# Gates of the expert lookup: hi and lo weights side by side in one product, one-hots from single-input operations, GELU kept in PSUM

## The chip, the cores and the metric

One core of one Trainium2 chip runs the whole program. The metric is the device time of one execution in microseconds (us), and smaller is better. The engines that matter here are TensorE (PE in the rows; its weight loads are PEld), VectorE (DVE), ScalarE (ACT) and GpSimd (POOL). SP issues most of the DMAs. SBUF is the working memory, PSUM the small memory into which TensorE writes its products, in eight banks of 512 float32 per partition.

## The reference

The program is two blocks of a network on 256 tokens of width 1024. Only the last part of the second block, a lookup of experts called PEER, is touched by the change. Cut to what matters:

```python
v1, i1 = lax.top_k(s1, 16)                 # 8 heads, 128 keys in each of two lists
v2, i2 = lax.top_k(s2, 16)
cand_s = v1[..., :, None] + v2[..., None, :]
cand_i = i1[..., :, None] * 128 + i2[..., None, :]
top_s, pos = lax.top_k(cand_s, 16)         # 16 experts per head, 128 per token
experts = take_along_axis(cand_i, pos)
gates = softmax(top_s)
u = u_tab[experts]                         # 16384 experts of width 1024
act = gelu(einsum('ced,cd->ce', u, x)) * gates
out = einsum('ce,ced->cd', act, v_tab[experts])
```

So each token has 128 gates, each for one of 128 x 128 experts (first index i1, second index i2).

## The kernel before, in words

The kernel does not gather. It computes the GELU of all 16384 experts for all 256 tokens (stage "U"), multiplies by a dense array of gates that is zero for experts that were not selected, and multiplies the result with the whole second table (stage "V"). The dense array is `big`, 128 partitions (i2) by 128 (i1) by 256 tokens, float32 in SBUF.

Stage U is the loop of `peer` over pairs of i1 (64 iterations). Each iteration loads two blocks of the table (L1507), splits each into a rounded part and a rest (ScalarE L1509; the rest on VectorE for three eighths and on GpSimd for five eighths, both L1511) and lets TensorE make 48 matmuls of 256 columns into one PSUM bank (L1514, recorded at L163). Then come GELU and the product with the gates: for the `n` tokens whose gates are there already, ScalarE writes GELU into an SBUF tile `tmp` (L1518) and VectorE multiplies it into `big` (L1519). For the other tokens ScalarE writes GELU straight into `big` (L1521), and the gates are multiplied in later.

Selection and gates are a generator (`select`, which hands over to `gates` once per half of 128 tokens) that runs beside stage U: after each iteration `spend(2.81)` lets it do a few steps, and a group of four tokens in `gates` counts as 1.8, so about 1.56 groups are done per iteration. The order in time is: selection of the first half (before and at the start of stage U), 32 gate groups, selection of the second half, 32 gate groups. All of it is in order on each engine's queue; the tile framework may move an instruction within the queue when it plans the program, not while it runs.

For a token the gate array is a product: a matrix with a one at (slot, i2) against a matrix with the gate's weight at (slot, i1), summed over the 128 slots on the partitions. `hots` (L1465) makes these matrices for four tokens at once with four operations of VectorE on 128 x 512 float16, each with two SBUF inputs: the comparison with i1 (L1469), that times the upper part of the weight (L1470) and times its rest (L1471), and the comparison with i2 (L1472). The four tokens are interleaved, so a token's matrix has a step of four elements. `fill` (L1475) is done one group later: two accumulating matmuls of 128 columns per token, upper part and rest, into one PSUM bank (L1478, L1479, recorded at L163 as `y<-s`), then VectorE multiplies the first `n` rows of i1 (those whose GELU is there) into `big` (L1483) and ScalarE copies the other rows into `big` (L1485). Both write `big` with a step of 256 elements.

PSUM is two pools of four banks: `ps` for stage U's products, `acc` (tile name `y`) for the rest.

Of the kernel before, what the change touches and what calls it, by code (L numbers as in the profile page):

```python
# [8 lines left out]
F32 = mybir.dt.float32  # L9
# [4 lines left out]
F16 = mybir.dt.float16  # L14
AF = mybir.ActivationFunctionType
OP = mybir.AluOpType
# [3 lines left out]
P = 128  # L20
S = 256
# [26 lines left out]
PK = 128  # L48
# [6 lines left out]
class Net:  # L55
# [1338 lines left out]
    def select(self, s12, eT):  # L1394


        nc, V = self.nc, self.nc.vector
        tk = self.tk
        for t in range(T):
# [44 lines left out]
            pe = self.acc.tile([P, 512], F32, name="y").rearrange("p (j s) -> p j s", j=4)  # L1444
            for j in range(3):
                self.transpose(pe[:, j], et[:, j].rearrange("p h s -> p (h s)"))
            e = eT[:, :, t * P:t * P + P]
            V.tensor_copy(e[:, 0:2], pe[:, 0:2])
            f = tk.tile([P, P], F32, name="cand")
            V.tensor_scalar(f, pe[:, 2], 2.0 ** 15, None, op0=OP.mult)  # L1450
            V.tensor_copy(e[:, 2], f)
            V.tensor_tensor(e[:, 3], f, e[:, 2], op=OP.subtract)
            yield 2.0
            yield from self.gates(t, eT)

    def gates(self, t, eT):


        nc, V = self.nc, self.nc.vector
        if t == 0:  # L1460
            buf = self.tk.tile([P, 2048], F32, name="s", bufs=2)
            self.tmp.append(buf[:, :512])
            self.hot = buf[:, 512:].bitcast(F16).rearrange("p (r j n q) -> p r j n q", r=2, n=PK, q=4)

        def hots(t4):  # L1465

            o2, oh, ol = (self.hot[:, t4 // 4 % 2, j] for j in range(3))
            of = lambda j: eT[:, j, None, t4:t4 + 4].to_broadcast([P, PK, 4])
            V.tensor_tensor(ol, self.iota4, of(0), op=OP.is_equal)  # L1469
            V.tensor_tensor(oh, ol, of(2), op=OP.mult)  # L1470
            V.tensor_tensor(ol, ol, of(3), op=OP.mult)  # L1471
            V.tensor_tensor(o2, self.iota4, of(1), op=OP.is_equal)  # L1472
            return o2, oh, ol

        def fill(t4, o2, oh, ol):  # L1475
            pg = self.acc.tile([P, 512], F32, name="y").rearrange("p (q n) -> p q n", q=4)
            for q in range(4):
                self.mm(pg[:, q], o2[:, :, q], oh[:, :, q], True, False)  # L1478
                self.mm(pg[:, q], o2[:, :, q], ol[:, :, q], False, True)  # L1479
            n = self.ready  # L1480
            sl = self.big[:, :, t4:t4 + 4].rearrange("p i t -> p t i")
            if n:
                V.tensor_tensor(sl[:, :, :n], pg[:, :, :n], sl[:, :, :n], op=OP.mult)  # L1483
            if n < PK:
                nc.scalar.copy(sl[:, :, n:], pg[:, :, n:])  # L1485
            self.gated = t4 + 4
        late = None
        for t4 in range(t * P, t * P + P, 4):
            h = hots(t4)
            if late:  # L1490
                fill(*late)
            late = (t4,) + h
            yield 1.8
        fill(*late)

    def peer(self, hn, big, out):

        nc, V = self.nc, self.nc.vector
        U, W = self.io["peer_u"], self.io["peer_v"]
        self.big, self.ready, self.gated = big, 0, 0  # L1500
        self.tmp = [self.tk.tile([P, 512], F32, name="tmp")]
        self.phase("U")
        for i in range(0, PK, 2):
            ps = self.psum((P, 2, S))
            for q in range(2):
                ur = self.up.tile([P, KB, P], F32, name="raw")
                nc.sync.dma_start(ur, U[i + q])  # L1507
                up = self.pp.tile([P, 2, KB, P], F32R, name="pair")
                nc.scalar.copy(up[:, 0], ur)  # L1509
                for eng, ks in ((V, slice(0, UD)), (nc.gpsimd, slice(UD, KB))):  # L1510
                    lo = eng.tensor_tensor(up[:, 1, ks], ur[:, ks], up[:, 0, ks].bitcast(F32), op=OP.subtract)  # L1511
                    at = lo if eng is V else at
                for k in range(KB):
                    self.mm3(ps[:, q], (up[:, 0, k], up[:, 1, k]), (hn[0][:, k], hn[1][:, k]), k == 0, k == 7)  # L1514
            n = self.gated
            if n:
                tmp = self.tmp[i // 2 % 2].rearrange("p (q s) -> p q s", q=2)[:, :, :n]
                nc.scalar.activation(tmp, ps[:, :, :n], AF.Gelu_apprx_tanh)  # L1518
                V.tensor_tensor(big[:, i:i + 2, :n], tmp, big[:, i:i + 2, :n], op=OP.mult)  # L1519
            if n < S:  # L1520
                nc.scalar.activation(big[:, i:i + 2, n:], ps[:, :, n:], AF.Gelu_apprx_tanh)  # L1521
            self.ready = i + 2
            with self.tc.issue_after(at.ins):
                self.spend(PACE)
        self.spend(1e6)
        self.phase("V")
        y = self.out_tiles()
        av = [self.tk.tile([P, 2, S], F32R, name=n) for n in ("eT", "tmp")]
        h = self.tk.tile([P, 2048], F32, name="s", bufs=2).rearrange("p (t d) -> p t d", t=T)
        nc.gpsimd.dma_start(h, self.h_dram)  # L1530
        for i in range(PK):
            vr = self.up.tile([P, D], F32, name="raw")
            nc.sync.dma_start(vr, W[i * P:(i + 1) * P])
            vp = self.pp.tile([P, 2, D], F32R, name="pair")
            self.split(vp[:, 0], vp[:, 1], vr)
            ah, al = av[i % 2][:, 0], av[i % 2][:, 1]
            self.split(ah, al, big[:, i])
            for t in range(T):
                ts = slice(t * P, t * P + P)
                for hf in range(2):  # L1540
                    cs = slice(hf * 512, hf * 512 + 512)
                    self.mm3(y[t][hf], (ah[:, ts], al[:, ts]), (vp[:, 0, cs], vp[:, 1, cs]), i == 0, i == PK - 1)
        for t in range(T):
            for hf in range(2):
                cs = slice(hf * 512, hf * 512 + 512)
                V.scalar_tensor_tensor(h[:, t, cs], y[t][hf], 2.0 ** -15, h[:, t, cs], op0=OP.mult, op1=OP.add)
        self.final(h, out)
# [22 lines left out]
def const_arrays():  # L1570
# [8 lines left out]
    for i in range(4):  # L1579
        sel4[32 * i, i] = 1  # L1580
    c["sel4"] = sel4
    c["iota4"] = np.broadcast_to(np.arange(P, dtype=np.float16)[:, None], (P, P, 4)).copy()
    c["iota16h"] = np.broadcast_to(np.arange(16, dtype=np.float16)[:, None], (P, 16, 16)).copy()
    c["iota128"] = np.broadcast_to(np.arange(P, dtype=f), (P, P)).copy()
    c["iota16"] = np.broadcast_to(np.tile(np.arange(16, dtype=f) - 16, T), (P, T * 16))
# [128 lines left out]
def block2(net, out):  # L1714
# [3 lines left out]
    with ExitStack() as ctx:  # L1718
# [9 lines left out]
        with ExitStack() as c3:  # L1728
# [5 lines left out]
            sel = net.side_pool("sel")  # L1734
            net.tk = sel.__enter__()
            s12 = [net.tk.tile([P, 2048], F32, name="s", bufs=2).rearrange("p (g n) -> p g n", g=16) for _ in range(T)]
            net.iota4 = net.tk.tile([P, PK, 4], F16, name="c_iota4")
            net.iota16 = net.tk.tile([P, 16, 16], F16, name="c_iota16")
            nc.gpsimd.dma_start(net.iota4, net.io["iota4"])
            nc.gpsimd.dma_start(net.iota16, net.io["iota16h"])  # L1740
            eT = net.tk.tile([P, 4, S], F16, name="eT")
            net.side, net.credit = net.select(s12, eT), 0
            net.peer_scores(hn, s12)
        big = pool("big", 1).tile([P, PK, S], F32, name="big")
# [81 lines left out]
```

## Time and profile before

| what | us |
|---|---|
| median of 3 runs | 2090.09 |
| lowest and highest | 2086.18, 2092.48 |
| the profiled execution, its own time | 2095.26 |
| its span, first to last instruction | 2093.5 |
| outside the span | 1.8 |
| stage with gates, from the first one-hot to the end of stage U | 1320 to 1730 |
| of it: gates of the first half, selection of the second, gates of the second | 146, 98, 166 |

The profiled execution is 5 us (0.25%) above the median. Over the span TensorE is busy 95%, VectorE 58%, ScalarE 38% and GpSimd 21%, but these shares are averages over stages. A stage is read by cutting it out of the span (busy time of each engine in a stretch), by the chain of waits in that stretch, and then by the durations and start times of the single instructions. In a row, "x64" is a count, "mean ns of one" includes any time in which an instruction had started and was held up, and "128x512 f16" is partitions by elements.

### The profile page before, as it was taken

The numbers are of one execution on the slowest core, as the hardware profiler recorded it, in microseconds if no ns is written. First come the engines' busy times: TensorE is split into PE (matmuls) and PEld (weight loads), VectorE is DVE, ScalarE is ACT, GpSimd is POOL, SyncE is SP. The second block draws the span as 40 slices with busy tenths as digits, with TensorE's granted clock in tenths as the row PEclk, the third lists the DMA queues.
The fourth block names the chain that finished last, engine by engine and source line by source line (L and its number), as shares of the span: only waits on it lengthen the run. The fifth ranks groups of instructions, "written<-read, shape, count | busy, mean of one in ns | idle before, by whom it ended". The sixth has DMA issues, their size and how long they took to land.

```text
span 2093.5 us, 32358 instructions
## 1 busy us (share of the span) xinstructions
PE 1987.4 (95%) x12820; PEld 1558.3 (74%) x12823; DVE 1210.6 (58%) x2475; ACT 794.6 (38%) x1248; POOL 434.2 (21%) x335
## 2 busy tenths in 40 slices
PE   6999999979999999997988999999999999999998
PEld 4967544438898854444866789999999998888886
DVE  3555211137885421114687569777999985555555
ACT  3343111124454211113433553555444444444443
POOL 1002000002332200000231034544665550000000
PEclk9999999999999899998998999999999999999999
DMA  9797799996785789996332361444564445555554
GB/s 388 293 403 268 273 395 391 396 374 229 283 288 175 276 315 395 395 392 258 139 109 96 121 255 32 161 142 147 167 191 152 141 152 191 191 190 191 187 189 148
DMA packets 155602, 496.13 MB, mean 237 GB/s; under 512 B 10145, under 2 KB 10561, under 8 KB 146865
## 3 DMA queue, kind: packets, MB, share of 16 engines
q1 hardware_dynamic: 152592, 483.42, 64.0%
q0 software_dynamic: 2848, 10.53, 1.3%
q8 instruction: 104, 1.70, 0.3%
q14 instruction: 58, 0.47, 0.1%
HBM read 486.30 MB, written 7.61 MB: 236 GB/s over the span
## 4 chain that ended last, share of the span: by engine, by line
PE 53%; DVE 8%; issue 2%; ACT 1%; POOL 1%; POOLq 0%; DVEq 0%; ACTq 0%
PE ps L163 27%; PE y L163 24%; DVE pair L1511 1%; PE y L1164 1%; DVE i L1412 0%; DVE hl L153 0%; DVE et L1435 0%; DVE ps L1157 0%; POOL hl L160 0%; ACT hl L151 0%; DVE pos L1423 0%; DVE v L1411 0%; PE ps L187 0%; DVE ps L1152 0%; DVE top L1422 0%
## 5 line engine op out<-in xcount | busy, mean ns | idle before, releaser
L163 PE MATMUL ps<-hn,pair 128*128 128x256 f32 x3072 | 384.9, 285 | 4.3 <-DVE pair L1511 4.2
L163 PEld LDWEIGHTS ps<-hn,pair 128*128 128x128 f32 x3072 | 375.3, 192 | 5.5 <-DVE pair L1511 5.0
L1511 POOL TENSOR_TENSOR pair<-raw,pair 128x640 fp32r<-128x640 f32 x128 | 235.8, 1849 | 158.9 <-ACT pair L1509 154.7
L163 PE MATMUL ps<-w,t 128*64 128x512 f32 x576 | 254.6, 595 | 5.4 <-DVE t L194 3.8
L163 PE MATMUL ps<-hl,t 128*64 128x512 f32 x576 | 254.2, 595 | 0.0
L151 ACT CAST hl<-w 128x2048 fp32r<-128x2048 f32 x79 | 150.1, 1903 | 137.7 <-PE ps L163 73.3
L153 DVE TENSOR_TENSOR pair<-raw,pair 128x1024 fp32r<-128x1024 f32 x128 | 156.8, 1225 | 67.2 <-ACT pair L151 67.2
L163 PE MATMUL y<-pair,tmp 128*128 128x512 f32 x768 | 189.5, 395 | 0.0
L163 PE MATMUL y<-pair,eT 128*128 128x512 f32 x768 | 186.3, 391 | 0.0
L163 PEld LDWEIGHTS y<-pair,tmp 128*128 128x128 f32 x768 | 144.4, 188 | 33.9
L163 PEld LDWEIGHTS ps<-w,t 128*64 128x64 f32 x576 | 76.3, 137 | 125.2 <-issue 117.7
L163 PEld LDWEIGHTS y<-pair,eT 128*128 128x128 f32 x768 | 144.3, 188 | 32.3
L1509 ACT CAST pair<-raw 128x1024 fp32r<-128x1024 f32 x128 | 134.2, 1051 | 64.4 <-DMA raw<-peer_u 25.1
L153 DVE TENSOR_TENSOR hl<-w,hl 128x2048 fp32r<-128x2048 f32 x51 | 118.5, 2323 | 51.4 <-ACT hl L151 48.3
L151 ACT CAST pair<-raw 128x1024 fp32r<-128x1024 f32 x128 | 133.8, 1045 | 1.1 <-issue 1.1
L711 DVE TENSOR_TENSOR t<-t,ps 128x512 f32<-128x512 f32 x16 | 11.0, 688 | 210.8 <-PE ps L163 210.8
L163 PE MATMUL ps<-hl,a 128*128 128x256 f32 x1008 | 130.2, 287 | 1.8 <-ACT hl L151 1.8
L330 POOL TENSOR_TENSOR ln_st<-ln_st,c_mhalf 128x1 f32<-128x1 f32 x8 | 6.3, 793 | 602.4 <-ACT ln_st L327 602.4
L163 PEld LDWEIGHTS ps<-hl,a 128*128 128x128 f32 x1008 | 124.0, 191 | 6.1 <-ACT hl L151 2.0
L163 PE MATMUL ps<-a,hl 128*128 128x256 f32 x864 | 106.8, 284 | 2.2 <-DVE a L153 1.3
L163 PEld LDWEIGHTS ps<-a,hl 128*128 128x128 f32 x864 | 104.6, 192 | 5.0 <-ACT t L368 1.5
L163 PEld LDWEIGHTS ps<-hl,t 128*64 128x64 f32 x576 | 74.4, 137 | 37.6 <-issue 37.1
(423 smaller groups left out, 3070.7 us busy)
## 6 DMA issues: line engine op xcount, KB each, us to landing
raw<-peer_u SPq DMA_DIRECT2D x128, 512.0 KB, 3.5
raw<-peer_v SPq DMA_DIRECT2D x128, 512.0 KB, 3.4
w<-ada_w SPq DMA_DIRECT2D x35, 1024.0 KB, 9.9
w<-moe_w_gate SPq DMA_DIRECT2D x24, 1024.0 KB, 16.2
w<-moe_w_up SPq DMA_DIRECT2D x24, 1024.0 KB, 14.1
w<-moe_w_down SPq DMA_DIRECT2D x24, 1024.0 KB, 14.1
hl<-moe_w_gate SPq DMA_DIRECT2D x24, 1024.0 KB, 14.3
hl<-moe_w_up SPq DMA_DIRECT2D x24, 1024.0 KB, 14.1
```

Of the source, the lines that this page charges most:

```text
L151: nc.scalar.copy(hi, src)
L153: nc.vector.tensor_tensor(lo, src, hi.bitcast(F32), op=OP.subtract)
L163: self.nc.tensor.matmul(out, lhsT=lhsT, rhs=rhs, start=start, stop=stop, skip_group_check=True)
L330: nc.gpsimd.tensor_tensor(st[:, 3:4], st[:, 2:3], self.mhalf[:, 0:1], op=OP.pow)
L711: nc.vector.tensor_tensor(hid, hid, pu, op=OP.mult)
L1164: self.nc.tensor.matmul(py[32 * q:32 * q + 32, :S], lhsT=self.s5_ct[ct][:, 4 * i + q], rhs=ab[q % 2][:, x, ri], start=j == 0, stop=j == 3, ...
L1509: nc.scalar.copy(up[:, 0], ur)
L1511: lo = eng.tensor_tensor(up[:, 1, ks], ur[:, ks], up[:, 0, ks].bitcast(F32), op=OP.subtract)
```

## The change

The one-hots of a token are made by single-input operations: a float16 row 0 to 127 (`iota4`, now without the four-fold repetition) is compared with a per-partition number of the token, and for the two weighted matrices multiplied by a second per-partition number in the same instruction. That is 12 operations on 128 x 128 float16 per group instead of four on 128 x 512. The token's numbers (`eT`) are kept in float32 for one half of the tokens at a time, and the upper part of a weight is rounded to float16 first.

Upper part and rest lie side by side, so that a token's gate is one matmul of 256 columns. A group's products then take two PSUM banks, two tokens in each. For each bank ScalarE copies the rest's half to SBUF (`low`), VectorE adds it to the upper half, in PSUM for the first `n` rows, multiplies those into `big`, and adds the other rows straight into `big`.

In stage U GELU is written back to PSUM, and VectorE's product with `big` reads it there; the SBUF tiles `tmp` go.

```diff
-            e = eT[:, :, t * P:t * P + P]
-            V.tensor_copy(e[:, 0:2], pe[:, 0:2])
-            f = tk.tile([P, P], F32, name="cand")
-            V.tensor_scalar(f, pe[:, 2], 2.0 ** 15, None, op0=OP.mult)
-            V.tensor_copy(e[:, 2], f)
-            V.tensor_tensor(e[:, 3], f, e[:, 2], op=OP.subtract)
+            V.tensor_copy(eT[:, 0:2], pe[:, 0:2])
+            f = tk.tile([P, 2, P], F32, name="cand")
+            half = f[:, 1].bitcast(F16)[:, :P]
+            V.tensor_scalar(f[:, 0], pe[:, 2], 2.0 ** 15, None, op0=OP.mult)
+            V.tensor_copy(half, f[:, 0])
+            V.tensor_copy(eT[:, 2], half)
+            V.tensor_tensor(eT[:, 3], f[:, 0], eT[:, 2], op=OP.subtract)
...
-            o2, oh, ol = (self.hot[:, t4 // 4 % 2, j] for j in range(3))
-            of = lambda j: eT[:, j, None, t4:t4 + 4].to_broadcast([P, PK, 4])
-            V.tensor_tensor(ol, self.iota4, of(0), op=OP.is_equal)
-            V.tensor_tensor(oh, ol, of(2), op=OP.mult)
-            V.tensor_tensor(ol, ol, of(3), op=OP.mult)
-            V.tensor_tensor(o2, self.iota4, of(1), op=OP.is_equal)
-            return o2, oh, ol
-
-        def fill(t4, o2, oh, ol):
-            pg = self.acc.tile([P, 512], F32, name="y").rearrange("p (q n) -> p q n", q=4)
+            hot = self.hot[:, t4 // 4 % 2]
             for q in range(4):
-                self.mm(pg[:, q], o2[:, :, q], oh[:, :, q], True, False)
-                self.mm(pg[:, q], o2[:, :, q], ol[:, :, q], False, True)
+                e = [eT[:, j, (t4 + q) % P:(t4 + q) % P + 1] for j in range(4)]
+                V.tensor_scalar(hot[:, q, 0], self.iota4, e[1], None, op0=OP.is_equal)
+                V.tensor_scalar(hot[:, q, 1], self.iota4, e[0], e[2], op0=OP.is_equal, op1=OP.mult)
+                V.tensor_scalar(hot[:, q, 2], self.iota4, e[0], e[3], op0=OP.is_equal, op1=OP.mult)
+            return hot
+
+        def fill(t4, hot):
+
             n = self.ready
-            sl = self.big[:, :, t4:t4 + 4].rearrange("p i t -> p t i")
-            if n:
-                V.tensor_tensor(sl[:, :, :n], pg[:, :, :n], sl[:, :, :n], op=OP.mult)
-            if n < PK:
-                nc.scalar.copy(sl[:, :, n:], pg[:, :, n:])
+            for u in range(2):
+                pg = self.acc.tile([P, 512], F32, name="y").rearrange("p (q j n) -> p q j n", q=2, j=2)
+                for q in range(2):
+                    self.mm(pg[:, q].rearrange("p j n -> p (j n)"), hot[:, 2 * u + q, 0],
+                            hot[:, 2 * u + q, 1:3].rearrange("p j n -> p (j n)"), True, True)
+                at = t4 + 2 * u
+                sl = self.big[:, :, at:at + 2].rearrange("p i t -> p t i")
+                low = self.lows[:, u]
+                nc.scalar.copy(low, pg[:, :, 1])
+                if n:
+                    V.tensor_tensor(pg[:, :, 0, :n], pg[:, :, 0, :n], low[:, :, :n], op=OP.add)
+                    V.tensor_tensor(sl[:, :, :n], pg[:, :, 0, :n], sl[:, :, :n], op=OP.mult)
+                if n < PK:
+                    V.tensor_tensor(sl[:, :, n:], pg[:, :, 0, n:], low[:, :, n:], op=OP.add)
...
-                tmp = self.tmp[i // 2 % 2].rearrange("p (q s) -> p q s", q=2)[:, :, :n]
-                nc.scalar.activation(tmp, ps[:, :, :n], AF.Gelu_apprx_tanh)
-                V.tensor_tensor(big[:, i:i + 2, :n], tmp, big[:, i:i + 2, :n], op=OP.mult)
+                nc.scalar.activation(ps[:, :, :n], ps[:, :, :n], AF.Gelu_apprx_tanh)
+                V.tensor_tensor(big[:, i:i + 2, :n], ps[:, :, :n], big[:, i:i + 2, :n], op=OP.mult)
...
-            net.iota4 = net.tk.tile([P, PK, 4], F16, name="c_iota4")
+            net.iota4 = net.tk.tile([P, PK], F16, name="c_iota4")
...
-            eT = net.tk.tile([P, 4, S], F16, name="eT")
+            eT = net.tk.tile([P, 4, P], F32, name="eT")
```

## Rows read from the trace of the kernel before

**Rows 1.** Busy time in three stretches: first gates, selection, second gates.
```profile
1320.00:1466.00 146.00, 146.00 (x1223) 144.79 (x1222) 103.27 (x226) 78.30 (x109) 71.64 (x41) 1.00 0.45 149
1466.00:1564.00 98.00, 96.27 (x787) 95.68 (x785) 94.80 (x297) 46.81 (x69) 64.93 (x41) 0.98 0.56 178
1564.00:1730.00 166.00, 165.05 (x1371) 162.41 (x1370) 154.74 (x237) 71.15 (x127) 91.14 (x46) 1.00 0.46 150
```
Columns: stretch and length in us, then PE, PEld, DVE, ACT and POOL busy us with counts, granted clock, DMA share, GB/s.

**Rows 2.** Chain of waits by line, of the first gate stretch and of the second.
```profile
by line: PE ps L163 80.5%; PE y L163 19.5%
...
by line: PE ps L163 66.3%; PE y L163 16.3%; issue 3.5%; DVE pair L1511 3.5%; DVE big L1483 2.7%; DVE s L1472 2.4%; DVE s L1471 1.7%; DVE s L1469 1.6%; DVE s L1470 1.0%; DVE big L1519 0.8%; PE y L187 0.3%; DVEq L1483 0.0%
```

**Rows 3.** Chain of waits in time order, 1340 to 1360: one gate group, one iteration's matmuls.
```profile
1350.50 0.95 PE y L163 x8
1351.45 5.75 PE ps L163 x48
```

**Rows 4.** VectorE's groups by line, 1320 to 1730: busy us, mean ns; then idle before.
```profile
L1511 DVE TENSOR_TENSOR pair<-raw,pair 128x384 fp32r<-128x384 f32 x117 | 80.7, 690 | 8.9 <-ACT pair L1509 8.4
L1483 DVE TENSOR_TENSOR big<-y,big 128x48 f32<-128x48 f32 (+31 forms) x64 | 48.6, 784 | 1.6 <-PE y L163 0.9 <-ACT pair L1509 0.5
L1470 DVE TENSOR_TENSOR s<-s,eT 128x512 f16<-128x512 f16 x64 | 41.7, 655 | 0.0
L1472 DVE TENSOR_TENSOR s<-c_iota,eT 128x512 f16<-128x512 f16 x64 | 40.3, 630 | 0.0
L1469 DVE TENSOR_TENSOR s<-c_iota,eT 128x512 f16<-128x512 f16 x64 | 35.7, 557 | 10.0 <-PE y L163 9.9
L1471 DVE TENSOR_TENSOR s<-s,eT 128x512 f16<-128x512 f16 x64 | 33.6, 536 | 0.6
L1519 DVE TENSOR_TENSOR big<-tmp,big 128x256 f32<-128x256 f32 (+20 forms) x29 | 19.1, 659 | 16.4 <-ACT tmp L1518 16.4
L1519 DVE TENSOR_TENSOR big<-s,big 128x256 f32<-128x256 f32 (+21 forms) x29 | 16.6, 572 | 16.9 <-ACT s L1518 16.9
```

**Rows 5.** Timeline of VectorE: one-hots back to back. Columns: start us, length us, instruction.
```profile
1323.16 0.41 DVE L1469 TENSOR_TENSOR s<-c_iota,eT 128x512 f16<-128x512 f16 x1
1323.50 0.41 DVE L1472 TENSOR_TENSOR s<-c_iota,eT 128x512 f16<-128x512 f16 x1
```

**Rows 6.** Per-partition operands: a line's min/median/max ns, and timeline rows of runs back to back.
```profile
L1099 DVE TENSOR_SCALAR a<-s_tt,s5s x16: 340/348/845, 516.5 to 619.0; 128x256 f32<-128x256 f16 x16
...
555.42 0.61 DVE L1099 TENSOR_SCALAR a<-s_tt,s5s 128x256 f32<-128x256 f16 x2
...
219.75 1.37 DVE L761 TENSOR_SCALAR t<-ps,ada_sc,ada_sh 128x128 f32<-128x128 f32 x4 [4.61 <-PE ps L163]
...
L860 DVE TENSOR_SCALAR a<-a x8: 410/414/424, 532.4 to 631.7; 128x512 f32<-128x512 f32 x8
...
L860 DVE TENSOR_SCALAR cosT<-cosT x1: 294/294/294, 171.6 to 171.6; 128x256 f32<-128x256 f32 x1
```

**Rows 7.** Timeline of VectorE: two-input operations on PSUM, the second waiting for the first.
```profile
1151.53 0.69 DVE L1152 TENSOR_TENSOR ps<-ps,raw 128x512 f32<-128x512 f32 x1
...
1152.26 0.43 DVE L1153 TENSOR_TENSOR ps<-ps,t 128x256 f32<-128x256 f32 x1
```

**Rows 8.** Timeline of VectorE: the gates' product with big, first and last groups.
```profile
1330.18 0.52 DVE L1483 TENSOR_TENSOR big<-y,big 128x48 f32<-128x48 f32 x2
...
1716.77 2.58 DVE L1483 TENSOR_TENSOR big<-y,big 128x496 f32<-128x496 f32 x2
```

**Rows 9.** Timeline of GpSimd, then of VectorE, 1299.5 to 1302.
```profile
1298.13 3.25 POOL L1511 TENSOR_TENSOR pair<-raw,pair 128x640 fp32r<-128x640 f32 x2
...
1299.03 1.11 DVE L1435 TENSOR_REDUCE et<-oh 128x32 f32<-128x512 f16 x1
1300.04 1.38 DVE L1416 CAST fi<-i 128x32 f16<-128x32 uint32 x1
...
1301.74 0.53 DVE L1511 TENSOR_TENSOR pair<-raw,pair 128x384 fp32r<-128x384 f32 x1
```

More of the change, by code (lines that the diff above doesn't have):

```diff
@@ L1461, in gates @@
             buf = self.tk.tile([P, 2048], F32, name="s", bufs=2)
-            self.tmp.append(buf[:, :512])
-            self.hot = buf[:, 512:].bitcast(F16).rearrange("p (r j n q) -> p r j n q", r=2, n=PK, q=4)
+            self.lows = buf[:, :512].rearrange("p (r q n) -> p r q n", r=2, q=2)
+            self.hot = buf[:, 512:].bitcast(F16).rearrange("p (r q j n) -> p r q j n", r=2, q=4, j=3)
         def hots(t4):
-            o2, oh, ol = (self.hot[:, t4 // 4 % 2, j] for j in range(3))
-            of = lambda j: eT[:, j, None, t4:t4 + 4].to_broadcast([P, PK, 4])
@@ L1491, in gates @@
                 fill(*late)
-            late = (t4,) + h
+            late = (t4, h)
             yield 1.8
@@ L1500, in peer @@
         self.big, self.ready, self.gated = big, 0, 0
-        self.tmp = [self.tk.tile([P, 512], F32, name="tmp")]
         self.phase("U")
@@ L1581, in const_arrays @@
     c["sel4"] = sel4
-    c["iota4"] = np.broadcast_to(np.arange(P, dtype=np.float16)[:, None], (P, P, 4)).copy()
+    c["iota4"] = np.broadcast_to(np.arange(P, dtype=np.float16), (P, P)).copy()
     c["iota16h"] = np.broadcast_to(np.arange(16, dtype=np.float16)[:, None], (P, 16, 16)).copy()
```

## The prediction

> **What bounds the kernel now.** I read busy time by stretch first, then the chain of waits, then single instructions. The change lives between 1320 us (first one-hot) and 1730 us (end of stage U), 410 us of the span. In the stretch of the first gates TensorE is busy all 146 us and VectorE 103; in the selection and in the second gates TensorE is still busy for 98 to 99%, but VectorE is too: 94.8 of 98 and 154.7 of 166 us [rows 1]. The reader should see that two engines are near their limit, and that over the 410 us VectorE has only 410 - 353 = 57 us free. The chain says the same: the first gate stretch is TensorE alone, stage U's products for 80.5% and the gates' for 19.5%; in the second a sixth of the chain is VectorE and issue [rows 2]. So an edit that takes from TensorE and gives to VectorE gains only until VectorE's 57 us are used up.
>
> **TensorE's part.** A group's eight gate matmuls take 0.95 us, 0.119 each; stage U's 48, with twice the columns, take 5.75, or 0.120 each [rows 3]. So 256 columns cost what 128 do, and four matmuls per group instead of eight save 0.475 us: 64 groups, 30 us. This is the whole gain on offer where TensorE sets the pace. The granted clock is 1.00 (the upper level, 2.4 GHz) in both gate stretches [rows 1], so nothing is to be had from the clock.
>
> **VectorE, one-hots.** Now: four operations on 512 float16 elements, starting 0.34 us after each other with a length of 0.41 [rows 5]; a group costs 4 x 0.335 = 1.34 us when nothing holds it up. After: 12 operations on 128 elements, four with one per-partition number and eight with two. The trace has no float16 result of this form, so I bound it. What streaming costs: the same kind without such numbers takes 0.414 us on 512 and 0.294 on 256 float32 elements, 0.47 ns an element, 0.06 us for 128; float16 may be anywhere between nothing and that. What starting costs: two runs of L1099 (one number, 256 elements) take 0.61 us together and 0.348 alone, so they start 0.26 apart, less 0.12 of streaming: 0.14. Four of L761 (two numbers, 128 elements from PSUM) take 1.37 us; with a last one of some 0.40 they start 0.32 apart, less 0.13 of streaming from PSUM (1.04 ns an element, next paragraph): 0.19 [rows 6]. So a group costs 4 x 0.14 + 8 x 0.19 = 2.08 us and up to 12 x 0.06 = 0.72 more: 2.08 to 2.80, taken in the middle as 2.44, since the stream lies in neither row's type. Against 1.34 that is +1.10 us (0.74 to 1.46), for 64 groups **+70 us** (47 to 93). Fewer elements, but three times as many starts, and each number adds to a start.
>
> **VectorE, fill.** Now one product per group. It reads and writes `big` with a step of 256: two in a row take 0.52 us at 48 elements and 2.58 at 496 [rows 8], some 2.4 ns an element and 0.07 per start. Its 48.6 us over 64 groups [rows 4] put the mean number of ready rows at n = 68 (12 in the first group, 124 in the last), so 0.07 + 4 x 68.5 x 0.0024 = 0.73 us. After, for each pair of tokens: an addition of 2n elements in PSUM, 1.04 ns an element with 0.155 to start (0.69 us at 512 elements, 0.43 at 256), and what needs its result starts 0.04 after its end [rows 7]: 0.195 + 0.142 = 0.34. Then the strided product, 0.07 + 137 x 0.0024 = 0.40. Then an addition of the other 119 elements into strided `big`, which was ScalarE's copy: no row of VectorE shows a strided write alone, so between the contiguous 1.04 ns and the product's 2.4, with 0.085 to start: 0.21 to 0.37, middle 0.29. Together 1.03 per pair, 2.05 per group (1.89 to 2.21), +1.32 us, for 64 groups **+85 us** (74 to 95). The second addition exists because upper part and rest no longer accumulate in PSUM; TensorE did it within its matmuls.
>
> **VectorE, what waits are in its busy time.** One-hots were busy 151 us for 256 operations [rows 4] that take 0.41 unhindered [rows 5]: 46 us of being held up. L1511 has 80.7 us for 117 that take 0.53 when free [rows 4, 9]: 18. With a little for L1519, 70 us in all. What holds them is GpSimd's L1511, about one operation of 1.6 us for each block: the cast L1416 starts at 1300.04 and ends at 1301.42, when GpSimd's second one ends (1298.13 + 3.25 = 1301.38), while the reduction L1435 inside the same GpSimd work takes 1.11 us without a hitch [rows 9]. L1416 has one input, in SBUF, as the new one-hots have; L1099, also of one input, has a longest of 845 ns against a median of 348 [rows 6]. So I let the one-hots wait as before: GpSimd issues as many operations, and each can hold VectorE once. GELU from PSUM frees L1519's wait, at most some 8 us, and the additions on PSUM don't wait; against that VectorE, busy throughout, meets more of GpSimd's operations in the first stretch than now. I leave the 70 us as they are, with 0 and 123 as ends (0.96 us for each of the 128 GpSimd operations, what the second stretch has now: 44 us for 46 [rows 1]).
> The Trainium skill, "SBUF — State Buffer", section on SBUF's two separate sides, says that VectorE and GpSimd share a port pair under an exclusive lock, and that a VectorE operation in a two-port mode takes it as one with two SBUF inputs does. By that rule the new one-hots wait too, and the sum stays as it is; the trace agrees, with L1416's 1.38 us [rows 9]. If only two-input operations waited, the first rival would hold.
>
> **Edits with one answer.** ScalarE copies 256 elements per pair instead of the rows that are left, and is busy 43 to 54% of the stretches [rows 1]; covered, and if VectorE has to wait for a copy, that lies in the idle share below. GELU into PSUM keeps a bank until VectorE has multiplied; four banks, one per iteration, cover it. The numbers in float32, one more cast, the smaller constant and its DMA before the stage: under 1 us. The gates of a group now take two of the four `acc` banks, one group ahead as before.
>
> **The sum.** VectorE's 353 us become 353 + 70 + 85 = 508 us of work in a stage of 410. VectorE sets the pace, and TensorE's 30 us are not seen. In the selection, where it is near its limit now, it is busy 97% [rows 1]; 508 / 0.97 = 524 us, **+114 us**. Nothing in stage V can take this back: its first matmul needs all gates of its row of `big`. On the profiled execution that is 2095.3 + 114 = 2209; on the median, 0.25% lower, 2090.1 + 114 = 2204 us.
>
> **Rivals.**
> *One-hots that don't wait.* If single-input operations, and GELU from PSUM, escape GpSimd's hold altogether, 70 us go: 438 / 0.97 = 452, +42 us, 2132. For it: L1435 did not wait. Against it: L1416 did.
> *TensorE stays the bound (the other side: faster).* Place: VectorE's one-hots. If a one-hot starts well below 0.2 us after the last, VectorE keeps under TensorE's 410 - 30 = 380 us, and 30 us are gained: 2060. The point: without waits 283 us (353 - 70) + 85 of fill leave 12 for the one-hots on top of their present 86, so 98 / 768 = 0.13 us each, and no waits at all. For it: L1469 and L1472 start only 0.34 apart for 512 elements, 0.10 per start if a float16 element streams in 0.47 ns too [rows 5]. Against it: both rows with per-partition numbers start dearer [rows 6]. The Trainium skill, "VectorE: DVE Perf Modes", section on the TRN2 errata, gives 58 cycles and a quarter of the elements for such an operation, an estimate of 0.09 us, which is below this point; it does not price the per-partition numbers, and rows 6 speak against it.
> *Both ends low.* One-hots at 2.08, fill at 1.89, no waits: 353 + 47 + 74 - 70 = 404 us, no change that can be told, 2088.
> *Both ends high.* One-hots 2.80, fill 2.21 and waits of 123 us: 353 + 93 + 95 + 53 = 594, / 0.97 = 612, +202 us, 2292. VectorE would also wait for ScalarE's copies, which are queued behind GELUs that wait for TensorE.
>
> **How the numbers follow.** Forecast 0.58 (its own range 2160 to 2245); no waits 0.17; both high 0.10; TensorE-bound 0.10; both low 0.05. Measured differences under 0.3% can't be told from none. Faster 0.10, same 0.05, slower 0.85. The range 2105 to 2270 leaves out the TensorE case, the low case and half of the high one.
>
> **What would show it.** Between the first one-hot and the end of stage U: a stretch of 480 to 580 us instead of 410; VectorE busy 95% or more also in the first gate stretch, TensorE near 75 to 80%; in the chain VectorE's lines in place of TensorE's. One-hots 0.17 to 0.25 us apart, some of them over 1 us, ending with a GpSimd operation. Gate matmuls still 0.12 us with 256 columns. If the one-hots start 0.13 us or less apart and none is long, the sum falls; if the stretch shrinks to 380, TensorE was the bound throughout.

## The result, and the profile after

| | us |
|---|---|
| before, median of 4 runs (lowest, highest) | 2091.28 (2086.18, 2095.69) |
| after, median of 4 runs (lowest, highest) | 2214.03 (2212.54, 2218.81) |
| ratio, 95% interval | 1.0583 [1.056, 1.0607] |
| profiled execution of after, its span | 2215.03, 2213.3 |

The change makes the kernel 5.8% slower. The forecast was 2204, the range 2105 to 2270. The profiled executions differ by 2215.0 - 2095.3 = 120 us, and nearly all of it lies in the stage with gates.

Busy time of after in three stretches: gates of the first half, selection of the second, gates of the second (columns as in rows 1).

```profile
1316.00:1510.00 194.00, 155.56 (x1156) 144.60 (x1156) 186.08 (x598) 75.11 (x137) 73.02 (x45) 0.92 0.37 120
1510.00:1620.00 110.00, 97.51 (x752) 93.90 (x751) 107.25 (x351) 47.15 (x76) 59.36 (x39) 0.95 0.47 154
1620.00:1848.00 228.00, 171.89 (x1223) 160.14 (x1223) 220.69 (x650) 83.30 (x156) 70.66 (x44) 0.86 0.34 112
```

The stage takes 194 + 110 + 228 = 532 us instead of 410 [rows 1]. VectorE is busy for 514 of them, 96 to 98% in every stretch; TensorE, which was busy throughout, has fallen to 425, 80%. The granted clock, 1.00 in both gate stretches before, is 0.92 and 0.86: TensorE now has gaps, and in parts of these stretches it is granted the lower level (1.2 GHz). VectorE is idle for only 18 of the 532 us, which bounds what that can have cost. The chain of waits of the first gate stretch, all TensorE before [rows 2], is now mostly VectorE:

```profile
by line: DVE s L1472 18.7%; DVE s L1473 17.1%; DVE s L1471 14.1%; PE ps L163 11.3%; DVE pair L1517 11.1%; DVE big L1492 9.5%; issue 7.7%; DVE big L1490 3.3%; DVE y L1489 3.0%; DVE big L1524 1.3%; DVE et L1435 0.5%; ACT pair L1515 0.5%; ACT 
```

The second gate stretch has the same picture: VectorE's lines make nearly three quarters of its chain, TensorE's under a fifth.

The groups by line, from 1300 to 1860 us. L1471 is the comparison with i2 (one number per partition), L1472 and L1473 the two weighted one-hots (two numbers); L1489, L1490 and L1492 are the addition in PSUM, the product into `big` and the addition into `big`; L1517 is the rest of a table block, L1524 the product with GELU. They answer to rows 4; the row of L163 is TensorE's gate matmuls.

```profile
L1473 DVE TENSOR_SCALAR s<-c_iota,eT 128x128 f16<-128x128 f16 x256 | 108.0, 424 | 0.0
L1472 DVE TENSOR_SCALAR s<-c_iota,eT 128x128 f16<-128x128 f16 x256 | 104.4, 410 | 0.0
L1471 DVE TENSOR_SCALAR s<-c_iota,eT 128x128 f16<-128x128 f16 x256 | 98.4, 386 | 5.5 <-PE y L163 5.4
L1517 DVE TENSOR_TENSOR pair<-raw,pair 128x384 fp32r<-128x384 f32 x124 | 93.3, 759 | 8.0 <-ACT pair L1515 7.8
L1490 DVE TENSOR_TENSOR big<-y,big 128x24 f32<-128x24 f32 (+35 forms) x128 | 57.6, 451 | 0.1
L163 PE MATMUL y<-s 128*128 128x256 f16 x256 | 50.4, 289 | 48.1 <-DVE big L1492 47.0 <-DVE s L1473 0.5
L1492 DVE TENSOR_TENSOR big<-y,s 128x232 f32<-128x232 f32 (+35 forms) x128 | 47.2, 373 | 0.0
L1489 DVE TENSOR_TENSOR y<-y,s 128x24 f32<-128x24 f32 (+35 forms) x128 | 36.0, 302 | 0.4 <-ACT s L1487 0.4
L1524 DVE TENSOR_TENSOR big<-ps,big 128x256 f32<-128x256 f32 (+40 forms) x58 | 24.6, 428 | 1.3 <-ACT ps L1523 1.1
```

The one-hots are busy 108.0 + 104.4 + 98.4 = 310.8 us instead of 151.3. In the timeline of VectorE and GpSimd, 1700 to 1704 us, one sees both halves of that:

```profile
1700.38 0.25 DVE L1471 TENSOR_SCALAR s<-c_iota,eT 128x128 f16<-128x128 f16 x1
1700.55 0.31 DVE L1472 TENSOR_SCALAR s<-c_iota,eT 128x128 f16<-128x128 f16 x1
1700.77 0.31 DVE L1473 TENSOR_SCALAR s<-c_iota,eT 128x128 f16<-128x128 f16 x1
1700.99 1.56 DVE L1471 TENSOR_SCALAR s<-c_iota,eT 128x128 f16<-128x128 f16 x1
1702.47 0.30 DVE L1472 TENSOR_SCALAR s<-c_iota,eT 128x128 f16<-128x128 f16 x1
1702.69 1.59 DVE L1473 TENSOR_SCALAR s<-c_iota,eT 128x128 f16<-128x128 f16 x1
...
1700.97 1.53 POOL L1517 TENSOR_TENSOR pair<-raw,pair 128x640 fp32r<-128x640 f32 x1 [2.22 <-ACT pair L1515]
1702.70 1.53 POOL L1517 TENSOR_TENSOR pair<-raw,pair 128x640 fp32r<-128x640 f32 x1 [0.20 <-ACT pair L1515]
```

Unhindered, the next operation starts 0.17 us after a one-hot with one number and 0.22 after one with two. The two long ones start with a GpSimd operation and end with it: 1700.99 + 1.56 = 1702.55 against 1700.97 + 1.53 = 1702.50.

Since durations overlap, I also added up VectorE's timeline from start to next start (an idle gap is left out). These sums reproduce the busy time of the stage, 353.3 us before and 514.2 after, and say where the 161 us come from:

| VectorE's work in the stage | before | after | difference | forecast |
|---|---|---|---|---|
| one-hots, unhindered | 85.4 (64 x 1.335) | 154.9 (64 x 2.42) | +69.5 | +70 |
| one-hots, held up | 49.9 | 91.5 | +41.6 | 0 |
| fill (L1483; L1489, L1490, L1492) | 44.6 | 103.3 | +58.7 | +85 |
| rest of the table, held up too (L1511; L1517) | 73.7 | 77.9 | +4.2 | 0 |
| product with GELU (L1519; L1524) | 33.1 | 20.1 | -13.0 | up to -8, taken as 0 |

### The profile page after: what moved, and what is told of

It reads as the page before. It is cut to its first block, busy times and chain, and to the rows that moved or that the text cites. A ratio compares the mean times of both kernels' runs of the same rounds, so it can differ in the third digit from the quotient of the medians.

```text
span 2213.3 us, 32902 instructions
## 1 busy us (share of the span) xinstructions
PE 2007.9 (91%) x12566; PEld 1553.7 (70%) x12567; DVE 1365.8 (62%) x3309; ACT 803.5 (36%) x1312; POOL 408.6 (18%) x335
## 4 chain that ended last, share of the span: by engine, by line
PE 38%; DVE 24%; issue 3%; ACT 2%; POOL 1%; POOLq 0%; ACTq 0%; DVEq 0%
PE y L163 20%; PE ps L163 16%; DVE pair L1517 3%; DVE s L1472 3%; DVE s L1473 3%; DVE s L1471 3%; DVE big L1490 1%; DVE big L1492 1%; PE y L1164 1%; DVE y L1489 1%; DVE big L1524 1%; DVE et L1435 1%; DVE i L1412 1%; DVE pos L1423 1%; DVE hl L153 0%
## 5 line engine op out<-in xcount | busy, mean ns | idle before, releaser
L163 PE MATMUL ps<-hn,pair 128*128 128x256 f32 x3072 | 430.6, 300 | 52.7 <-DVE pair L1517 29.3
L163 PEld LDWEIGHTS ps<-hn,pair 128*128 128x128 f32 x3072 | 406.7, 206 | 64.5 <-ACT big L1526 27.7
L1517 POOL TENSOR_TENSOR pair<-raw,pair 128x640 fp32r<-128x640 f32 x128 | 211.2, 1654 | 284.1 <-ACT pair L1515 231.2
L163 PE MATMUL ps<-w,t 128*64 128x512 f32 x576 | 254.6, 595 | 5.4 <-DVE t L194 3.8
L163 PE MATMUL ps<-hl,t 128*64 128x512 f32 x576 | 254.2, 595 | 0.0
L163 PE MATMUL y<-pair,eT 128*128 128x512 f32 x768 | 187.9, 394 | 6.0 <-DVE eT L153 6.0
L163 PE MATMUL y<-pair,tmp 128*128 128x512 f32 x768 | 190.2, 396 | 0.0
L163 PEld LDWEIGHTS y<-pair,eT 128*128 128x128 f32 x768 | 145.7, 190 | 38.5 <-DVE eT L153 6.4
L163 PEld LDWEIGHTS y<-pair,tmp 128*128 128x128 f32 x768 | 144.7, 188 | 34.5
L163 PEld LDWEIGHTS ps<-w,t 128*64 128x64 f32 x576 | 76.3, 137 | 125.3 <-issue 117.5
L163 PE MATMUL ps<-hl,a 128*128 128x256 f32 x1008 | 130.2, 287 | 1.8 <-ACT hl L151 1.8
L163 PEld LDWEIGHTS ps<-hl,a 128*128 128x128 f32 x1008 | 124.0, 191 | 6.1 <-ACT hl L151 2.0
L163 PE MATMUL ps<-a,hl 128*128 128x256 f32 x864 | 107.3, 285 | 1.4 <-DVE a L153 1.1
L163 PEld LDWEIGHTS ps<-a,hl 128*128 128x128 f32 x864 | 105.3, 193 | 3.8 <-DVE a L153 1.3
L1473 DVE TENSOR_SCALAR s<-c_iota,eT 128x128 f16<-128x128 f16 x256 | 108.0, 424 | 0.0
```

The lines of the kernel that those rows point to most:

```text
L163: self.nc.tensor.matmul(out, lhsT=lhsT, rhs=rhs, start=start, stop=stop, skip_group_check=True)
L1473: V.tensor_scalar(hot[:, q, 2], self.iota4, e[0], e[3], op0=OP.is_equal, op1=OP.mult)
```

## The experiments

There are three kinds: single parts of the change, its two suspected costs taken away, and two remedies. Each is compared with the kernel before on the same chip; a ratio above 1 is slower.

| run | median us | ratio | 95% interval |
|---|---|---|---|
| gelu_only | 2107.48 | 1.0063 | 1.0045 to 1.0081 |
| hots_only | 2151.47 | 1.0282 | 1.0257 to 1.0308 |
| fill_only | 2113.83 | 1.0094 | 1.0073 to 1.0116 |
| o2_in_rows | 2112.29 | 1.0080 | 1.0061 to 1.0098 |
| after_no_gpsimd | 2104.64 | 1.0055 | 1.0039 to 1.0072 |
| before_no_gpsimd | 2087.73 | 0.9969 | 0.9954 to 0.9984 |
| after_constants | 2104.50 | 1.0051 | 1.0034 to 1.0068 |
| after_both_away | 2055.85 | 0.9821 | 0.9789 to 0.9852 |
| pairs | 2077.26 | 0.9932 | 0.9916 to 0.9947 |
| gelu_swap | 2088.97 | 0.9984 | 0.9974 to 0.9994 |
| pairs_swap | 2073.06 | 0.9904 | 0.9887 to 0.9922 |
| after_swap | 2206.19 | 1.0543 | 1.0522 to 1.0564 |

### One part alone: GELU in PSUM

```diff
-                tmp = self.tmp[i // 2 % 2].rearrange("p (q s) -> p q s", q=2)[:, :, :n]
-                nc.scalar.activation(tmp, ps[:, :, :n], AF.Gelu_apprx_tanh)
-                V.tensor_tensor(big[:, i:i + 2, :n], tmp, big[:, i:i + 2, :n], op=OP.mult)
+                nc.scalar.activation(ps[:, :, :n], ps[:, :, :n], AF.Gelu_apprx_tanh)
+                V.tensor_tensor(big[:, i:i + 2, :n], ps[:, :, :n], big[:, i:i + 2, :n], op=OP.mult)
```

> The kernel before with one part of the change: GELU is written back to PSUM and multiplied into big from there. Theory (VectorE's product with big no longer waits for GpSimd, and VectorE sets the pace only in the selection and the second gate stretch): L1519's 35.7 us of busy time fall to about 25, the 410 us between the first one-hot and the end of stage U shrink by 0 to 6 us, 2085 to 2091 in all. Rival (a PSUM bank kept until the product is made delays TensorE): 2095 or more, with waits of PE for ps on that line.

Measured: 2107.48, slower by 0.6%, a miss. The prediction had put this edit among those with one answer. The waits of ScalarE and of VectorE in this run (engine, line, what it waited for: us, times, longest), 1316 to 1860 us:

```profile
ACT big L1520 <- DVE big L1518: 57.1, 33, 4.0
DVE pair L1511 <- ACT pair L1509: 31.2, 26, 2.0
```

The first row does not exist before. ScalarE runs two activations on a bank: GELU of the first tokens, left in PSUM (L1517), and GELU of the later tokens into `big` (L1520). Between them VectorE's product now reads the same bank, and the second activation waits until it has done so. Before, the two engines wrote the same parts of `big` without such a wait, so it is the shared bank that the program guards here. The next cast of a table block (L1509) is queued behind it on ScalarE, so VectorE waits 31.2 us for casts instead of 8.4 [rows 4]. The Trainium skill, "PSUM — Partial Sum Buffer", section "PSUM bank collisions raise a hardware error", says that two engines must not touch a bank at once, two readers included, and that accesses are to be guarded by bank; the program here keeps to that, and the trace agrees with 57.1 us of such a wait.

### One part alone: the one-hots, and the fill

hots_only has the new one-hots, but two accumulating matmuls of 128 columns and the old fill; fill_only has the old, interleaved one-hots with one matmul of 256 columns and the new fill. Both have GELU in PSUM.

```diff
 hots_only, in fill:
-                    self.mm(pg[:, q].rearrange("p j n -> p (j n)"), hot[:, 2 * u + q, 0],
-                            hot[:, 2 * u + q, 1:3].rearrange("p j n -> p (j n)"), True, True)
...
+                self.mm(pg[:, q], hot[:, q, 0], hot[:, q, 1], True, False)
+                self.mm(pg[:, q], hot[:, q, 0], hot[:, q, 2], False, True)
...
 fill_only, in fill:
+                    r = self.hot[:, t4 // 4 % 2]
+                    self.mm(pg[:, q], r[:, 0, :, 2 * u + q], r[:, 1:3, :, 2 * u + q], True, True)
```

> One-hots as in the changed kernel (12 single-input operations, hi and lo side by side, GELU in PSUM), but hi and lo accumulate in PSUM by two matmuls of 128 columns and the fill is the old one. Theory (12 starts with per-partition numbers cost 2.42 us a group instead of 1.34, and more of them are held by GpSimd): VectorE's 353 us become 353 - 10 + 69 + some 40 of holds = 452, at 97% 466 us instead of 410: 2147. Rival (one-hots are cheap, the fill is the cost): 2095 or less.

> One product of 256 columns per token and the fill of the changed kernel (copy of the rest, two additions, two products a group), GELU in PSUM, but the one-hots by the old four operations, interleaved by four. Theory (the additions and the split product cost VectorE some 66 us more, with holds between the old and the new amount): 353 - 10 + 66 + 0 to 30 = 409 to 439, at 97% 421 to 453: 2101 to 2133. With hots_only the two parts should then sum to less than the change's +123, since VectorE's 57 free us are used by each alone but only once by both. Rival (the fill is hidden, the one-hots are the cost): 2060 to 2075, TensorE's 30 us gained.

Measured: 2151.47 and 2113.83, close to the theory's 2147 and inside its 2101 to 2133. Against gelu_only these are 44 and 6 us, together 50; both at once, the changed kernel, cost 107. Most of the gap is VectorE's free time. From the first one-hot to the end of stage U it is busy 381 of 424 us in gelu_only, 454 of 468 in hots_only, 423 of 433 in fill_only and 511 of 529 in the changed kernel: each part alone could use the 43 us that gelu_only has free, both together only once. The rest is that the two parts' work does not add up either, 73 and 42 us alone and 130 together.

The two runs also show what TensorE pays. Rows of its timeline in hots_only, then in fill_only:

```profile
1379.10 1.07 PE L163 MATMUL y<-s 128*128 128x128 f16 x16
```

```profile
1376.83 2.01 PE L163 MATMUL y<-s 128*128 128x256 f16 x8
```

Matmuls are pipelined, so I take the mean length of one off each row and divide the remainder by the others. With a token's one-hots contiguous, 16 matmuls of 128 columns are (1.07 - 0.22) / 15 = 0.057 us apart. With four tokens interleaved, 8 matmuls of 256 columns are (2.01 - 0.40) / 7 = 0.23 apart, twice the 0.119 of 128 columns before [rows 3]. So 256 columns do not cost what 128 do. What made the eight matmuls of before cost 0.95 us is the interleaving, and the changed kernel's gain on TensorE comes from the contiguous one-hots, whether hi and lo are side by side or not.

### Is it the weights' layout?

```diff
-            V.tensor_tensor(o2, self.iota4, of(1), op=OP.is_equal)
+            V.tensor_tensor(o2, self.iota1[:, None].to_broadcast([P, 4, PK]), eT[:, 1, t4:t4 + 4, None].to_broadcast([P, 4, PK]), op=OP.is_equal)
...
```

This is gelu_only with the one-hot that TensorE loads as weights (i2) written contiguous for each token; the streamed ones stay interleaved.

> gelu_only, and one of the four one-hot operations (the comparison with i2, which TensorE loads as weights) writes each token's 128 columns side by side instead of interleaved by four; its inputs are then broadcast in the last dimension. Theory (a gate matmul of 128 columns takes 0.119 us because the interleaved weights load slowly, 0.118 a load): a group of eight falls from 0.95 to about 0.7 us, the first gate stretch by up to 8 us, while VectorE pays 0.2 to 0.3 us a group, which shows in the second stretch: between 2080 and 2092. Rival (load time is the same in rows): 2090 to 2100.

Measured: 2112.29, no gain over gelu_only's 2107.48, a miss. The mean of the gate matmuls (1310 to 1760 us) has hardly moved, 296 ns in gelu_only and 292 here:

```profile
L163 PE MATMUL y<-s 128*128 128x128 f16 x512 | 71.1, 292 | 11.4 <-DVE s L1472 6.5 <-DVE s L1471 4.8
```

In hots_only, where the streamed operand is contiguous too, it is 221. The starts say the same: 16 of these matmuls in a row take 2.01 us here, 2.05 in gelu_only and 1.07 in hots_only. That leaves the streamed operand's step. The run `pairs` below halves the step of both operands.

### The two costs on VectorE taken away

after_no_gpsimd and before_no_gpsimd leave out GpSimd's part of the rest of each table block (five eighths of it), and the matmuls read another part of the tile in its place. after_constants makes the one-hots from four constants in place of the token's numbers, so that its gates are not those of the reference. after_both_away does both.

```diff
 the two no_gpsimd runs, in the loop of stage U (the matmuls' edit left out):
-                for eng, ks in ((V, slice(0, UD)), (nc.gpsimd, slice(UD, KB))):
+                for eng, ks in ((V, slice(0, UD)),):
 after_constants, in hots:
-                e = [eT[:, j, (t4 + q) % P:(t4 + q) % P + 1] for j in range(4)]
+                e = [3.0, 5.0, 0.5, 0.25]
```

> The changed kernel without GpSimd's five eighths of the rest of the table's rounding (left out of the computation; the matmuls read other parts of the tile instead, so TensorE, ScalarE and the DMAs do the same). Theory (some 115 us of VectorE's 514 busy us are operations held up by GpSimd): 514 - 115 = 399 us against TensorE's 380, the stage shrinks from 532 to 405 to 425 us: 2085 to 2110. Rival (the holds cost little, the work itself is the bound): 2180 or more.

> The kernel before with the same part of GpSimd's work left out. Theory (TensorE sets the pace there and the holds, some 70 us, mostly lie in VectorE's free time): the stage shrinks only in the selection and the second gates, by 5 to 15 us: 2075 to 2085. Rival (the holds set the pace of the kernel before too): 2040 or less.

> The changed kernel, but the one-hots compare and multiply with constants in the instruction instead of the token's per-partition numbers (so the gates are not the right ones); same count, same elements. Theory (each per-partition number adds some 63 ns to a start: 20 of them a group, 1.26 us): 64 x 1.26 = 81 us less of VectorE's work, stage 450: 2130. Rival (the number of operations is the price, not their operands): 2205 or more.

> The changed kernel with both: constants in the one-hots and GpSimd's part of the rest left out. Theory (VectorE falls to some 514 - 115 - 81 = 318 us, so TensorE sets the pace and its 256 saved matmuls show): stage 380 to 390 us, 2060 to 2070, under both kernels. Rival (256 columns cost more than 128, or something else holds the stage): 2090 or more.

Measured: 2104.64, 2087.73, 2104.50 and 2055.85. Only the first lies in its theory's range; the second is 3 us above it, the third 26 below the one forecast, the fourth 4 below its range. Without GpSimd's operations the changed kernel gets 109 us faster, the kernel before 5. Durations of L1473, smallest, median and largest ns, without GpSimd:

```profile
L1473 DVE TENSOR_SCALAR s<-c_iota,eT x256: 281/307/343, 1311.9 to 1722.0; 128x128 f16<-128x128 f16 x128
```

No one-hot is held any more (in the changed kernel the longest takes 1730 ns). Start to start, the 768 one-hots take 155.5 us in this run, which is the unhindered price of the table above, measured apart from the holds. So single-input operations on SBUF do wait for GpSimd. From the first one-hot to the end of stage U, VectorE's busy time falls from 511 to 399 us without GpSimd's operations, 112 less, and in the kernel before from 353 to 281, 72 less. Those 72 us lay beside TensorE's work: the chain of the kernel before without GpSimd is all TensorE, and 5 us are what they cost.

With constants the median one-hot falls from 248 and 307 to 181 to 182 ns, and one starts 0.10 us after the last, not 0.17 and 0.22:

```profile
1405.32 0.18 DVE L1471 TENSOR_SCALAR s<-c_iota 128x128 f16<-128x128 f16 x1
1405.42 0.18 DVE L1472 TENSOR_SCALAR s<-c_iota 128x128 f16<-128x128 f16 x1
1405.52 0.18 DVE L1473 TENSOR_SCALAR s<-c_iota 128x128 f16<-128x128 f16 x1
```

So each per-partition number costs some 0.06 us per instruction. 768 starts then take 77 us instead of 155. The run is 26 us faster than expected: the one-hots' holds fell too, from 91 to 141 - 77 = 64 us (141 is their start-to-start sum in this run), and in a shorter stage VectorE's idle time fell from 18 to 10.6 us.

With both away, busy time in the stage, then the chain of waits by line (1316 to 1700 us) and one of its pieces:

```profile
1310.00:1690.00 380.00, 380.00 (x3164) 373.49 (x3164) 333.12 (x1598) 203.43 (x373) 9.14 (x9) 1.00 0.51 173
...
by line: PE ps L163 88.2%; PE y L163 11.8%; PE y L187 0.1%
...
1347.08 0.89 PE y L163 x8
```

TensorE is busy all 380 us, the 410 - 30 of the rival "TensorE stays the bound", at a granted clock of 1.00, and VectorE has 47 us free. Eight matmuls of 256 contiguous columns take 0.89 us, 0.11 each. The rival's mechanism is real; what decided against it is the price of a one-hot and the holds. The Trainium skill, "VectorE: DVE Perf Modes", section on the TRN2 errata, gives a one-hot of 128 elements an estimate of 0.09 us and a matmul of n columns n + 6 cycles, an estimate of 0.056 us for 128 columns at 2.4 GHz; the measured 0.10 with constants and 0.057 with a contiguous operand agree, and neither figure prices a per-partition number or an interleaved operand.

### A remedy for the matmuls: two tokens interleaved instead of four

```diff
-            self.hot = buf[:, 512:].bitcast(F16).rearrange("p (r j n q) -> p r j n q", r=2, n=PK, q=4)
+            self.hot = buf[:, 512:].bitcast(F16).rearrange("p (r j a n q) -> p r j a n q", r=2, j=3, a=2, q=2)
...
-                self.mm(pg[:, q], o2[:, :, q], oh[:, :, q], True, False)
-                self.mm(pg[:, q], o2[:, :, q], ol[:, :, q], False, True)
+                a, c = q // 2, q % 2
+                self.mm(pg[:, q], o2[:, a, :, c], oh[:, a, :, c], True, False)
+                self.mm(pg[:, q], o2[:, a, :, c], ol[:, a, :, c], False, True)
```

> The kernel before with one edit: a group's one-hots are interleaved by two tokens instead of four, so that the gate matmuls read with a step of 2 float16 elements (4 bytes) instead of 4 (8 bytes). VectorE's four operations keep 512 elements. Theory (the step of the streamed operand is what makes a gate matmul cost 0.119 us for 128 columns): a group of eight takes 0.46 to 0.6 us instead of 0.95, TensorE's work falls by 22 to 31 us, VectorE's 353 us stay below the rest, and the time is 2062 to 2075 us, faster than both kernels. Rival (any step other than one costs the same): 0.95 us as before and 2088 to 2097.

Measured: 2077.26, faster by 0.7%, 2 us beyond the upper end that the theory gave. Two pieces of its chain, 1340 to 1380 us, and busy time in its three stretches:

```profile
1346.55 0.48 PE y L163 x8
1347.03 5.80 PE ps L163 x48
...
1316.00:1466.00 150.00, 149.21 (x1366) 148.26 (x1367) 130.90 (x277) 86.25 (x122) 81.01 (x47) 1.00 0.46 160
1466.00:1564.00 98.00, 94.92 (x785) 93.38 (x784) 95.04 (x270) 45.60 (x67) 65.89 (x42) 1.00 0.55 184
1564.00:1711.00 147.00, 138.96 (x1235) 134.37 (x1235) 144.59 (x215) 62.82 (x115) 86.02 (x40) 1.00 0.45 151
```

A group's eight matmuls take 0.48 us instead of 0.95 [rows 3], as with contiguous one-hots. VectorE still makes its four operations, with medians of 414 to 426 ns (411 to 425 before). So a streamed float16 operand with a step of 4 bytes costs TensorE what a contiguous one does, and with a step of 8 bytes twice that. All of TensorE's 30 us are there, but only about half come out: in the second gate stretch VectorE is busy 144.6 of 147 us. Its one-hots take 153 us start to start, 18 more than before, with the same medians, so that is holds.

### A remedy for the wait: ScalarE's two activations in the other order

```diff
+            if n < S:
+                nc.scalar.activation(big[:, i:i + 2, n:], ps[:, :, n:], AF.Gelu_apprx_tanh)
             if n:
                 nc.scalar.activation(ps[:, :, :n], ps[:, :, :n], AF.Gelu_apprx_tanh)
                 V.tensor_tensor(big[:, i:i + 2, :n], ps[:, :, :n], big[:, i:i + 2, :n], op=OP.mult)
-            if n < S:
-                nc.scalar.activation(big[:, i:i + 2, n:], ps[:, :, n:], AF.Gelu_apprx_tanh)
```

It was made in gelu_only (gelu_swap), together with the two-fold interleaving (pairs_swap), and in the changed kernel (after_swap).

> The run gelu_only, with ScalarE's GELU of the later tokens (PSUM to big) issued ahead of the GELU that stays in PSUM, so that ScalarE never asks for a bank while VectorE's product still reads it. Theory (gelu_only was slower because ScalarE's second activation waited 57 us for VectorE's product on its bank, which delayed its casts and copies): that wait goes, VectorE's wait for the cast falls from 31 to about 8 us, and the time is 2085 to 2095. Rival (the longer stay of the bank, or the product's read of PSUM, is what costs): 2102 to 2109.

> Both edits in one kernel: one-hots interleaved by two, and GELU in PSUM with the later tokens' GELU issued first. If the step of the streamed operand is what costs TensorE and ScalarE's order is what cost gelu_only, the two add up: 2058 to 2075. If the streamed step costs nothing, as gelu_swap alone; if GELU in PSUM still costs 10 us or more, 2075 to 2085.

> The changed kernel with the same order of ScalarE's two activations as in gelu_swap. Theory (VectorE's work of 514 us sets the pace there, ScalarE's wait of 66 us in front of its second activation is not on the path): 2204 to 2214. Rival (that wait is part of the loss): 14 us or more are given back, 2190 to 2200.

Measured: 2088.97, 2073.06 and 2206.19, all as the theory had it. ScalarE's wait for VectorE is gone from gelu_swap; its waits, 1316 to 1860 us, are now for TensorE and for the group's product:

```profile
ACT big L1517 <- PE ps L163: 97.1, 56, 1.8
ACT big L1485 <- DVE big L1483: 55.8, 52, 2.8
```

VectorE's wait for the casts falls from 31.2 to 7.5 us. The 14 us that GELU in PSUM cost alone were that order. In the changed kernel ScalarE's second activation waited 66.0 us for VectorE's product, more than in gelu_only, but removing the wait gives back only some 8 us of 123 (the intervals of the two ratios overlap at their ends): there VectorE is the bound. pairs_swap is the fastest of all, 1.0% below the kernel before; its interval overlaps that of pairs, so what the swapped GELU adds to it is not settled.

## Why the prediction was right, and where not, point by point

**What bounds.** Right. VectorE has taken over in all three stretches, for the reason given: 57 us free, more than twice that added. The runs with one part alone show the same threshold: against gelu_only 44 and 6 us alone, 107 together.

**One-hots.** Right in kind and size. A group costs 2.42 us unhindered, forecast 2.44, of which the two rows with per-partition operands [rows 6] had given the starts. The working had 0.14 and 0.19 us for a start and 0.03 for the elements; measured are 0.17 and 0.22, and with constants 0.10. The kind of cost was read from rows; that the total came out within 1% is partly luck, since the share of the elements was the middle between nothing and 0.06 for want of a row.

**Fill.** Right in kind, too dear: 103.3 us against 44.6, +59 instead of +85, outside its own range of 74 to 95. All three operations of a pair were too dear, start to start: the addition in PSUM 0.22 us instead of 0.34, the product 0.35 instead of 0.40, the addition into `big` 0.24 instead of 0.29, together 0.81 instead of 1.03. The largest miss is the addition in PSUM: I took its start of 0.155 us and a wait for the result from two operations that depend on each other [rows 7]. In the changed kernel other work lies between, and an addition of 192 elements costs 0.27 us to the next start, 1.04 ns an element and 0.07:

```profile
1704.67 0.35 DVE L1489 TENSOR_TENSOR y<-y,s 128x192 f32<-128x192 f32 x1
1704.94 0.55 DVE L1517 TENSOR_TENSOR pair<-raw,pair 128x384 fp32r<-128x384 f32 x1
```

**Holds.** The rule was right, the size was not. L1416's 1.38 us [rows 9] did mean that single-input operations wait, and leaving GpSimd out shows it. The 70 us fit the kernel before, where leaving GpSimd out takes 72 us of VectorE's work away. But I let them stay 70, and they became 112 (91 in the one-hots, 20 in the table blocks), near the upper end of 123. The reason that the text itself gave for more, VectorE being busy throughout, carries in the main: one-hots longer than 1 us went from 18 to 35 in the first gate stretch, where VectorE had been free for 43 of 146 us [rows 1], and from 19 to 31 in the second. The additions on PSUM did not wait, as forecast (longest 425 ns).

**GELU in PSUM.** Wrong, without harm to the sum. "Four banks, one per iteration, cover it" looked at TensorE, which needs a free bank, and not at ScalarE, which needs the same bank a second time while VectorE reads it. Alone it costs 14 us; in the changed kernel all but some 8 us of it is covered by VectorE's work, though there TensorE too waits for a bank, 23.0 us until that second activation is done. The product itself got 13 us cheaper, since L1524, reading PSUM, is not held by GpSimd as L1519 was (longest 691 ns, 1907 before); the forecast had at most 8.

**TensorE's part.** The size was right (30 us: after_both_away's 380 us, and 64 groups at 0.47 us less in pairs), the reason wrong, so the size was luck. I set gate matmuls on interleaved float16 beside stage U's on contiguous operands of twice the columns [rows 3] and read the equal 0.12 us as a price that does not depend on columns. Two things differed between the rows, and they cancelled.

**The sum.** 353 + 161 = 514 us over 0.97 gives 530; the stage took 532. The forecast's 508 was as near as it was because fill was 26 us too high, and holds and the GELU product together 33 too low (41.6 + 4.2 - 13.0). That these two errors nearly cancel is luck.

## What to carry to other kernels

Before an edit moves work to an engine, add up what that engine has free in the very stage, and count its waits for GpSimd as work that grows with it. Small single-input operations are paid by the start, and each per-partition number adds to it: one operation over several tokens beats several over one, if the layout that it leaves is one that TensorE streams at full pace. When two rows show the same price for different sizes, look for the second thing in which they differ, here the step of an operand, since the cheap remedy may lie there.

## What the runs showed of the hardware that was not expected

- A float16 operand streamed with a step of 8 bytes costs TensorE 0.119 us for 128 columns [rows 3]; with a step of 4 bytes 0.06, and contiguous 0.057. Contiguous weights alone did not change the 0.119. Why the limit lies between 4 and 8 bytes, and whether the weights' step matters once the streamed one is small, was not tried.
- Each per-partition number of a VectorE operation adds some 0.06 us from one start to the next: 0.10 without, 0.17 with one, 0.22 with two.
- A hold by GpSimd costs an operation of 0.25 to 0.31 us up to another 1.4 us, and 64 groups lost 91.5 us that way, though GpSimd was busy only 203 of the stage's 532 us. Operations that read PSUM were not held (product with GELU: longest 691 ns, against 1907 when it read SBUF).
- The program makes ScalarE wait for a PSUM bank until VectorE has read its part of it, so that GELU written back in place puts VectorE's product between ScalarE's two activations: 57.1 us of waiting, gone when the order is turned round.
